# Four PSUM banks for the pairs' products, and a later spread of the next block's roots, in a hybrid decoder layer

## The chip, the cores and the metric

The kernel runs on one core of one Trainium2 chip. The metric is the time of one execution in microseconds (us). Every time below is from the chip: from the timed runs, or from one profiled execution of the kernel before. The engines are named as the profile names them: PE (TensorE, matmul) with PEld (its weight loads), DVE (VectorE), ACT (ScalarE), POOL (GpSimd) and SP (whose queue issues DMAs). PSUM, where matmuls put their sums, has eight banks here, and the kernel uses all eight.

## The reference, cut to what matters

One layer of a decoder, over 2048 prompt tokens and 64 sample tokens. Everything begins with an RMS norm of x and one large projection `w_in`; the three branches' results are weighted by sigmoid gates and summed.

```python
def _mixer_inputs(x, p):
    xn = _rmsnorm(x, p["norm_w"])            # x * rsqrt(mean(x*x) + eps) * w
    h = jnp.einsum("btd,de->bte", xn, p["w_in"])
    ...
    gates = jax.nn.sigmoid(g + p["b_gate"]).reshape(n, t, N_BRANCHES, D_MODEL)

def _merge(x, y_a, y_b, y_c, z_a, z_b, z_c, gates, p):
    a = jnp.einsum("bte,ed->btd", jax.nn.silu(z_a) * y_a, p["w_out_a"])
    b = jnp.einsum("bte,ed->btd", jax.nn.silu(z_b) * y_b, p["w_out_b"])
    c = jnp.einsum("bte,ed->btd", jax.nn.silu(z_c) * y_c, p["w_out_c"])
    m = gates[:, :, 0] * a + gates[:, :, 1] * b + gates[:, :, 2] * c
    return x + jnp.einsum("btd,de->bte", m, p["w_o"])
```

## The kernel before

The tokens are worked through in four blocks: three of 512 tokens, and a last one of 512 prompt and 64 sample tokens (576, in two chunks of 288). Each block goes through the same phases: keys and values, queries, attention and convolution, the chunk MLP, the gate phase, the output phase. Weights are fp32 and each is split into a high part `wh` (a cast on ACT, line 222) and a low part `wl` (a subtraction on DVE, line 223); a product is then three matmuls, `wh`·`xh`, `wh`·`xl` and `wl`·`xh`. The weights come by DMA into a ring of three `raw` tiles and are split two units ahead of use into a ring of four `wh`/`wl` tiles.

The change touches the gate phase. There are 24 gate tiles (8 output tiles for each of 3 branches). The first four are done one by one (`single`): 24 matmuls of 512 columns for the gate, a sigmoid, 12 matmuls for the branch's output (`merge`, lines 231 to 233), which DVE multiplies with the gate (line 897) and adds up (line 903). The other 20 are done in ten pairs (`pair`) by a scheme of the Strassen-Winograd kind, which forms two gate tiles for both halves of the tokens with seven products in place of eight. Each product is 12 matmuls (lines 929 to 931) of half the tokens, 256 columns (288 in the last block). POOL forms the sums of weights that the scheme needs (lines 154 to 164). The seven products, in the order in which PE does them, are named here by their right side: `11`, `t3`, `t2`, `t1`, `21`, `t4`, `22`. Each is put into one PSUM bank and read by additions: `11` by a copy on ACT (line 946), `t3` and `t2` by DVE lines 950 and 949 (949 first, since 950 adds its result), `t1` by 952 and 953, `21` by 955, `t4` by 956, `22` by 959. Before, the banks are S0, pv, S1, S0, S1, pv, S0 in that order; the product that comes to a bank must wait until the one before it in that bank has been read. The other five banks are a ring of three (`ps_mm`, tag `mm`), which the gate and merge matmuls use, and a ring of two (`ps_tp`), for transposes.

During the gate phase the next block's root mean squares are prepared (`xrstd`): per 128 tokens a DMA of x and a sum of squares on ACT (line 261), then the roots on POOL (`fin`, lines 218 and 219), then a spread of the roots over the partitions: transposes on PE (line 275) into `ps_tp`, and a copy on ACT (line 278). The roots are used at the end of the gate phase (line 296). For the block of 576 there are five pieces, the last of 64 tokens.

What sets the order: PE's instructions and the DMAs of SP stand in program order; a scheduler orders DVE, ACT and POOL. Side work is hung into PE's program with `later(delay, piece)`. The clock of these delays counts PE's work: a gate tile of 512 columns is 1.0, a merge 0.5, a product 0.25. `flush()` runs all that is pending at once; one stands in `single(2)`, at 4.0, since what follows needs the third branch.

Of the kernel before, what the change touches and what calls it, by code (L numbers as in the profile page):

```python
# [10 lines left out]
F32 = mybir.dt.float32  # L11
F32R = mybir.dt.float32r
AF = mybir.ActivationFunctionType
ALU = mybir.AluOpType
AX = mybir.AxisListType

P = 128
# [34 lines left out]
def trunk_kernel(ctx: ExitStack, tc: tile.TileContext, A, O):  # L52
# [7 lines left out]
    psum = ctx.enter_context(tc.tile_pool(name="psum", bufs=1, space=bass.MemoryType.PSUM))  # L60

    def ps_mm():
        return psum.tile([P, 512], F32, tag="mm", name="ps_mm", bufs=3)
# [22 lines left out]
    def later(delay, fn):  # L86
        heapq.heappush(pending, (clock[0] + delay, len(pieces)))
        pieces.append(fn)
# [6 lines left out]
    def flush():  # L95
        while pending:
            pieces[heapq.heappop(pending)[1]]()
# [89 lines left out]
    def take(name, j):  # L187
        i = taken[0]
        assert units[i] == (name, j), (units[i], name, j)
        taken[0] += 1  # L190
        split_to(i + 1 + ahead["splits"])
        w = ready[i]
        ready[i] = None
        return w
# [26 lines left out]
    def split(hi, lo, src):  # L221
        nc.scalar.copy(hi, src)  # L222
        nc.vector.tensor_tensor(lo, src, hi.bitcast(F32), ALU.subtract)  # L223

    def gemm_t(ps, w, kts, rh, rl, c0, c1):

        wh, wl = w
        o = ps[:, : c1 - c0]
        for k in range(kts):
            ws = slice(k * P, (k + 1) * P)  # L230
            nc.tensor.matmul(o, wh[:, ws], rh(k, c0, c1), start=k == 0, stop=False)  # L231
            nc.tensor.matmul(o, wh[:, ws], rl(k, c0, c1), start=False, stop=False)  # L232
            nc.tensor.matmul(o, wl[:, ws], rh(k, c0, c1), start=False, stop=k == kts - 1)  # L233
            if k % 2:
                tick((c1 - c0) / 512 * 0.25)
# [12 lines left out]
    def xrstd(sb):  # L248

        t0, _, chunks, _ = SBS[sb]  # L250
        n = chunks[-1][1]
        tiles = [(c, min(c + P, n)) for c in range(0, n, P)]
        st = {}
        st["r"] = res.tile([P, TMAX], F32, tag="acc", name="acc")[:, :n]
        r = small.tile([P, 8], F32, tag="xr", name="xr")

        def piece(j, c0, c1):
            w = c1 - c0
            x = raws.tile([P, WE], F32, tag="raw", name="xraw")[:w]
            nc.sync.dma_start(x, A["xn"][t0 * P + c0:t0 * P + c1])  # L260
            nc.scalar.activation(x, x, AF.Square, accum_out=r[:w, j:j + 1])

        def fin():
            for j0, j1, w in ((0, n // P, P), (n // P, len(tiles), n % P)):
                if w and j1 > j0:
                    rstd(r[:w, j0:j1], r[:w, j0:j1], j1 - j0, D)

        def spread():
            for t in (tiles[:4], tiles[4:]):
                if t:  # L270
                    ps = ps_tp()
                    b = t[0][0]
                    for c0, c1 in t:
                        w = c1 - c0
                        nc.tensor.transpose(
                            ps[:, c0 - b:c1 - b], r[:w, c0 // P:c0 // P + 1].broadcast_to([w, P]), ident[:w, :w]
                        )
                    nc.scalar.copy(st["r"][:, b:t[-1][1]], ps[:, : t[-1][1] - b])

        return st, [lambda j=j, c=c: piece(j, *c) for j, c in enumerate(tiles)] + [fin, spread]  # L280
# [54 lines left out]
    pair = [None]  # L335
# [535 lines left out]
    def keep(new, old):  # L871

        tc.keep_in_program_order(nc.scalar.dma_start(O[new][:, : P - TS, :], A[old][:, TS:, :]))

    def gate_phase(sb, br, xs):
        chunks = SBS[sb][2]
        n = chunks[-1][1]
        h = n // 2
        sums, last_sums = xs
        st = {}  # L880
        if sb + 1 < len(SBS):
            st, xpieces = xrstd(sb + 1)
            for j, p in enumerate(xpieces):
                later(0.5 + 0.75 * j, p)

        def bias(j):
            d, b = divmod(j, 3)
            return bg[:, 8 * b + d:8 * b + d + 1]

        def merge(j, t, wo):  # L890

            d, b = divmod(j, 3)
            brr = (lambda k, x, y: br[b][0][:, k, x:y], lambda k, x, y: br[b][1][:, k, x:y])
            for c0, c1 in chunks:
                pa = ps_mm()
                gemm_t(pa, wo, 4, *brr, c0, c1)
                nc.vector.tensor_tensor(t[:, c0:c1], pa[:, : c1 - c0], t[:, c0:c1], ALU.mult)  # L897
            if b == 0:
                st["acc"] = t
            else:  # L900
                acc = st["acc"]
                out = acc if b == 1 else st["m"][:, d, :n]
                nc.vector.tensor_tensor(out, acc, t, ALU.add)

        def single(j):
            wg = take("wt", 28 + j)
            t = tmp("t", [P, n])
            for c0, c1 in chunks:
                pg = ps_mm()
                gemm_t(pg, wg, KT, *xr, c0, c1)  # L910
                nc.scalar.activation(t[:, c0:c1], pg[:, : c1 - c0], AF.Sigmoid, bias=bias(j))
            if j == 2:
                flush()
                st["m"] = res.tile([P, KT, TMAX], F32, tag="mh", name="m")
                for q in range(2):
                    later(0.25 + 0.75 * q, lambda q=q: last_sums(q))
                if not sb:
                    later(4.0, lambda: keep("sk", "ck"))
                    later(12.0, lambda: keep("sv", "cvr"))
            merge(j, t, take("wout", j))  # L920

        def product(bank, w, half, r):

            o = psum.tile([P, 512], F32, tag=bank, name="pair" + bank, bufs=1)[:, :h]
            wh, wl = w
            rh, rl = sums[r]
            for k in range(4):
                ws = slice(half * H + k * P, half * H + (k + 1) * P)
                nc.tensor.matmul(o, wh[:, ws], rh(k), start=k == 0, stop=False)  # L929
                nc.tensor.matmul(o, wh[:, ws], rl(k), start=False, stop=False)  # L930
                nc.tensor.matmul(o, wl[:, ws], rh(k), start=False, stop=k == 3)  # L931
                if k % 2:
                    tick(h / 2048)
            return o

        def pair(j):

            add = nc.vector.tensor_tensor
            ta, tb, ca, cb = [tmp(x, [P, n]) for x in ("t", "t", "ca", "cb")]
            lo, hi = slice(0, h), slice(h, n)
            p1, u, u3, u5 = ca[:, lo], ca[:, hi], cb[:, lo], cb[:, hi]
            w = take("pair", (28 + j, 0))
            nc.scalar.copy(p1, product("S0", w, 0, "11"))
            p3 = product("pv", w, 1, "t3")
            w = take("pair", (28 + j, 1))
            add(u, product("S1", w, 0, "t2"), p1, ALU.add)  # L949
            add(u3, p3, u, ALU.add)  # L950
            p5 = product("S0", w, 1, "t1")
            add(u5, p5, u, ALU.add)
            add(tb[:, hi], p5, u3, ALU.add)
            w = take("pair", (28 + j, 2))
            add(ta[:, lo], product("S1", w, 0, "21"), p1, ALU.add)
            add(tb[:, lo], product("pv", w, 1, "t4"), u3, ALU.add)
            nc.scalar.activation(tb, tb, AF.Sigmoid, bias=bias(j + 1))
            w = take("pair", (28 + j, 3))
            add(ta[:, hi], product("S0", w, 0, "22"), u5, ALU.add)
            nc.scalar.activation(ta, ta, AF.Sigmoid, bias=bias(j))  # L960
            wh, wl = take("wouts", j)
            if j == 22:

                st["hi"] = res.tile([P, KT, TMAX], F32R, tag="ml", name="mhi")
                st["lo"] = [res.tile([P, 4, TMAX], F32R, tag="br0" + x, name="mlo" + x) for x in "hl"]
                for d in range(KT - 1):
                    part(d)
            merge(j, ta, (wh[:, :H], wl[:, :H]))
            merge(j + 1, tb, (wh[:, H:], wl[:, H:]))

        def part(d):
            split(st["hi"][:, d, :n], st["lo"][d // 4][:, d % 4, :n], st["m"][:, d, :n])

        for j in range(SINGLES):
            single(j)
        for j in range(SINGLES, 24, 2):
            pair(j)
        part(KT - 1)
        flush()
        if sb + 1 < len(SBS):  # L980
            for j, p in enumerate(xsplit(sb + 1, st)):
                later(0.25 + 0.75 * j, p)
        return st["hi"], st["lo"]
# [206 lines left out]
```

## Time and profile before

| | us |
|---|---|
| median of three timed runs | 2015.57 (2015.36 to 2016.91) |
| the profiled execution's own time | 2013.36 |
| its span, first to last instruction | 2011.6 |
| PE busy in the span | 1972.3 (98%) |
| DVE busy | 1365.2 (68%) |
| ACT busy | 945.1 (47%) |
| POOL busy | 335.0 (17%) |

The rows of the profile give an engine's busy time; for PE the ends of matmuls are modelled and overlap, so a wait is read more exactly from the distance between the starts of matmuls. A "wait" in the profile is idle time of an engine that ended with an event of another; PE and PEld are listed apart, so one stop of TensorE can stand in both lists. "Granted clock" is the share of TensorE's full speed: 1.00 is 2.4 GHz, 0.50 is 1.2 GHz.

### The profile page before, as it was taken

How to read it: one execution, taken by the hardware profiler on the slowest of the kernel's cores; microseconds unless marked ns; L12 is line 12 of the kernel's file. 1: busy time of each engine (PE TensorE's matmuls, PEld its weight loads, DVE VectorE, ACT ScalarE, POOL GpSimd, SP SyncE). 2: the span in 40 equal slices, each digit the busy share in tenths (PEclk: the TensorE clock that was granted, in tenths of full speed). 3: DMA queues.
4: the chain of work that ended last, by engine and by line, in shares of the span. 5: the costliest groups of instructions: out<-in, count | busy, mean ns of one | idle time of the engine just before them, and what ended most of it. 6: DMA issues, size and time to landing. Idle time of an engine off the chain costs nothing.

```text
span 2011.6 us, 30272 instructions
## 1 busy us (share of the span) xinstructions
PE 1972.3 (98%) x11771; PEld 1765.4 (88%) x11771; DVE 1365.2 (68%) x2367; ACT 945.1 (47%) x1679; POOL 335.0 (17%) x294
## 2 busy tenths in 40 slices
PE   6999999999999999999999998999999999999999
PEld 5888889998888889998888887999889999999999
DVE  5688377875588558777478736777647873587772
ACT  4775254442576344444367524444347743333340
POOL 2100024320100004440200002442020000133310
PEclk9999999999999999999999998999999999999999
DMA  6222233336222232226322223223622242222233
GB/s 209 90 79 84 84 126 115 102 115 224 95 73 74 94 114 101 101 95 207 129 84 74 87 76 123 97 95 115 229 87 56 62 114 69 71 82 87 95 101 109
DMA packets 85711, 212.44 MB, mean 106 GB/s; under 512 B 18224, under 2 KB 23344, under 8 KB 85552
## 3 DMA queue, kind: packets, MB, share of 16 engines
q1 hardware_dynamic: 85536, 209.53, 32.4%
q8 instruction: 92, 1.51, 0.3%
q10 hardware_dynamic: 32, 0.98, 0.1%
q14 instruction: 51, 0.42, 0.1%
HBM read 201.46 MB, written 10.00 MB: 105 GB/s over the span
## 4 chain that ended last, share of the span: by engine, by line
PE 89%; DVE 5%; ACT 4%; DMA 1%; issue 1%; POOL 1%; SPq 0%; ACTq 0%; DVEq 0%; POOLq 0%
PE ps_mm L231 18%; PE ps_mm L232 18%; PE ps_mm L233 18%; PE pairS L929 4%; PE pairS L930 4%; PE pairS L931 4%; DVE wl L223 3%; PE pairpv L930 2%; PE pairpv L929 2%; PE pairpv L931 2%; PE ps_mm L353 2%; PE ps_mm L352 2%; PE ps_mm L351 2%; ACT wh L222 2%; PE wideS L353 1%; PE wideS L352 1%
## 5 line engine op out<-in xcount | busy, mean ns | idle before, releaser
L223 DVE TENSOR_TENSOR wl<-raw,wh 128x1024 fp32r<-128x1024 f32 (+1 forms) x416 | 461.7, 1118 | 272.1 <-ACT wh L222 269.1
L222 ACT CAST wh<-raw 128x1024 fp32r<-128x1024 f32 (+1 forms) x416 | 354.7, 866 | 539.1 <-PE ps_mm L232 232.7
L231 PE MATMUL ps_mm<-xh,wh 128*128 128x512 f32 (+1 forms) x1280 | 460.2, 360 | 0.0
L233 PE MATMUL ps_mm<-xh,wl 128*128 128x512 f32 (+1 forms) x1280 | 451.7, 353 | 0.0
L232 PE MATMUL ps_mm<-xl,wh 128*128 128x512 f32 (+1 forms) x1280 | 451.6, 353 | 0.0
L233 PEld LDWEIGHTS ps_mm<-xh,wl 128*128 128x128 f32 x1280 | 241.0, 188 | 30.7
L232 PEld LDWEIGHTS ps_mm<-xl,wh 128*128 128x128 f32 x1280 | 241.5, 189 | 27.1
L231 PEld LDWEIGHTS ps_mm<-xh,wh 128*128 128x128 f32 x1280 | 241.3, 189 | 27.3
L222 ACT CAST wh<-s 128x512 fp32r<-128x512 f32 x120 | 70.9, 621 | 194.1 <-PE ps_mm L232 116.5
L929 PE MATMUL pairS<-xh,wh 128*128 128x256 f32 (+1 forms) x480 | 140.1, 292 | 8.1 <-DVE ca L949 7.9
L218 POOL TENSOR_SCALAR vr<-vssq 128x1 f32<-128x1 f32 (+1 forms) x17 | 5.4, 316 | 804.9 <-ACT vn L795 804.5
L931 PE MATMUL pairS<-xh,wl 128*128 128x256 f32 (+1 forms) x480 | 137.2, 286 | 0.0
L930 PE MATMUL pairS<-xl,wh 128*128 128x256 f32 (+1 forms) x480 | 137.1, 286 | 0.0
L231 PE MATMUL ps_mm<-mhi,wh 128*128 128x512 f32 (+1 forms) x320 | 112.5, 352 | 0.9 <-ACT mhi L222 0.9
L233 PE MATMUL ps_mm<-mhi,wl 128*128 128x512 f32 (+1 forms) x320 | 112.5, 352 | 0.0
L897 DVE TENSOR_TENSOR t<-ps_mm,t 128x512 f32<-128x512 f32 (+1 forms) x120 | 70.8, 593 | 58.5 <-PE ps_mm L233 57.3
L929 PEld LDWEIGHTS pairS<-xh,wh 128*128 128x128 f32 x480 | 91.2, 190 | 14.5 <-DVE ca L949 13.2
L154 POOL TENSOR_TENSOR s<-raw 128x512 f32<-128x512 f32 x40 | 56.8, 1419 | 243.1 <-DMA raw<-in_wt 192.2
L164 POOL TENSOR_TENSOR s<-raw,s 128x512 f32<-128x512 f32 x40 | 67.6, 1690 | 160.2 <-DVE wl L223 160.2
L930 PEld LDWEIGHTS pairS<-xl,wh 128*128 128x128 f32 x480 | 91.4, 190 | 1.2
L929 PE MATMUL pairS<-xsum,wh 128*128 128x256 f32 (+1 forms) x320 | 91.7, 287 | 0.0
L930 PE MATMUL pairS<-xsum,wh 128*128 128x256 f32 (+1 forms) x320 | 91.6, 286 | 0.0
(280 smaller groups left out, 4638.7 us busy)
## 6 DMA issues: line engine op xcount, KB each, us to landing
raw<-in_wt SPq DMA_DIRECT2D x208, 512.0 KB
raw<-in_wout SPq DMA_DIRECT2D x96, 256.0 KB
raw<-in_wn SPq DMA_DIRECT2D x40, 512.0 KB
raw<-in_wo SPq DMA_DIRECT2D x32, 512.0 KB
xraw<-in_xn SPq DMA_DIRECT2D x12, 512.0 KB
xt<-in_xt SPq DMA_DIRECT2D x24, 256.0 KB
out_yt<-xt SPq DMA_DIRECT2D x24, 256.0 KB
xbuf<-in_xt SPq DMA_DIRECT2D x16, 256.0 KB
```

The source lines that it names most:

```text
L164: add(combos["s2"], r0[:, H:], combos["s2"], ALU.subtract)
L222: nc.scalar.copy(hi, src)
L223: nc.vector.tensor_tensor(lo, src, hi.bitcast(F32), ALU.subtract)
L231: nc.tensor.matmul(o, wh[:, ws], rh(k, c0, c1), start=k == 0, stop=False)
L232: nc.tensor.matmul(o, wh[:, ws], rl(k, c0, c1), start=False, stop=False)
L233: nc.tensor.matmul(o, wl[:, ws], rh(k, c0, c1), start=False, stop=k == kts - 1)
L352: nc.tensor.matmul(o, xh[:, k, ts], wl, start=False, stop=False)
L353: nc.tensor.matmul(o, xl[:, k, ts], wh, start=False, stop=k == KT - 1)
L897: nc.vector.tensor_tensor(t[:, c0:c1], pa[:, : c1 - c0], t[:, c0:c1], ALU.mult)
L929: nc.tensor.matmul(o, wh[:, ws], rh(k), start=k == 0, stop=False)
L930: nc.tensor.matmul(o, wh[:, ws], rl(k), start=False, stop=False)
L931: nc.tensor.matmul(o, wl[:, ws], rh(k), start=False, stop=k == 3)
```

## The change

Two things. First, product `t1` goes into a buffer of the `mm` ring in place of S0, `21` into S0 in place of S1, and `22` into S1 in place of S0, so that the order of banks is S0, pv, S1, mm, S0, pv, S1. Second, the last two pieces of the next block's preparation (`fin` and the spread) are no longer due at 0.5 + 0.75·j with the others. They are hung in behind the flush of `single(2)`, at 2.0 and 6.0 after it.

```diff
@@ gate_phase
         if sb + 1 < len(SBS):
             st, xpieces = xrstd(sb + 1)
-            for j, p in enumerate(xpieces):
+            for j, p in enumerate(xpieces[:-2]):
                 later(0.5 + 0.75 * j, p)
+            st["roots"] = xpieces[-2:]
...
                 for q in range(2):
                     later(0.25 + 0.75 * q, lambda q=q: last_sums(q))
+
+                for q, p in enumerate(st.get("roots", [])):
+                    later(2.0 + 4.0 * q, p)
...
+        def bank_of(bank):
+            if bank == "mm":
+                return ps_mm()
+            return psum.tile([P, 512], F32, tag=bank, name="pair" + bank, bufs=1)
+
         def product(bank, w, half, r):
 
-            o = psum.tile([P, 512], F32, tag=bank, name="pair" + bank, bufs=1)[:, :h]
+            o = bank_of(bank)[:, :h]
...
-            p5 = product("S0", w, 1, "t1")
+            p5 = product("mm", w, 1, "t1")
...
-            add(ta[:, lo], product("S1", w, 0, "21"), p1, ALU.add)
+            add(ta[:, lo], product("S0", w, 0, "21"), p1, ALU.add)
...
-            add(ta[:, hi], product("S0", w, 0, "22"), u5, ALU.add)
+            add(ta[:, hi], product("S1", w, 0, "22"), u5, ALU.add)
```

Lines from 949 on of the kernel before are nine higher in the changed kernel (949 is 958 there), 929 to 931 are 938 to 940, and 897 and 903 are 898 and 904.

PE at the border between products `t1` and `21`, in the second pair of the first block, before (a name's number tells buffers apart; what an instruction waits for is behind it):

```order
L929 MATMUL pairS_2813<-xsum,wh 128x256
L930 MATMUL pairS_2813<-xsum,wh 128x256
L931 MATMUL pairS_2813<-xsum,wl 128x256
L929 MATMUL pairS_2832<-xh,wh 128x256 [waits DVE_49]
L930 MATMUL pairS_2832<-xl,wh 128x256
L931 MATMUL pairS_2832<-xh,wl 128x256
```

The same place now:

```order
L938 MATMUL ps_mm<-xsum,wh 128x256
L939 MATMUL ps_mm<-xsum,wh 128x256
L940 MATMUL ps_mm<-xsum,wl 128x256
L938 MATMUL pairS_2826<-xh,wh 128x256 [waits Activation_49]
L939 MATMUL pairS_2826<-xl,wh 128x256
L940 MATMUL pairS_2826<-xh,wl 128x256 [waits DVE_49]
```

The first matmul of `21` no longer waits for DVE (line 949, which reads S1) but for ACT; the third waits for DVE's low part of its weights.

DVE in the fifth pair of the first block, before:

```order
L223 TENSOR_TENSOR wl<-s_3234,wh 128x512
L949 TENSOR_TENSOR ca<-pairS_3319,ca 128x256
L223 TENSOR_TENSOR wl<-raw,wh 128x1024
L950 TENSOR_TENSOR cb<-pairpv,ca 128x256
L952 TENSOR_TENSOR cb<-pairS_3334,ca 128x256
```

and now:

```order
L223 TENSOR_TENSOR wl<-s_3234,wh 128x512
L958 TENSOR_TENSOR ca<-pairS_3319,ca 128x256
L223 TENSOR_TENSOR wl<-raw,wh 128x1024
L959 TENSOR_TENSOR cb<-pairpv,ca 128x256
L961 TENSOR_TENSOR cb<-ps_mm,ca 128x256
```

Nothing moved here: only the bank that line 961 reads is another. In the whole program DVE's order differs in one place, nine rows in the third block's sums for `t4` (lines 840 and 864), and POOL's and SP's orders do not differ at all.

PE around the flush of `single(2)` in the third block (the next block has five pieces), before:

```order
L231 MATMUL ps_mm<-xh,wh 128x512
L232 MATMUL ps_mm<-xl,wh 128x512
L233 MATMUL ps_mm<-xh,wl 128x512
L275 MATMUL ps_tp<-c_ident,xr 128x128 x4
L275 MATMUL ps_tp<-c_ident,xr 128x64
L231 MATMUL ps_mm<-br2h,wh 128x512
L232 MATMUL ps_mm<-br2l,wh 128x512
L233 MATMUL ps_mm<-br2h,wl 128x512
```

The transposes now stand in the second pair of that block, between products `21` and `t4`:

```order
L938 MATMUL pairS_11584<-xh,wh 128x256
L939 MATMUL pairS_11584<-xl,wh 128x256
L940 MATMUL pairS_11584<-xh,wl 128x256
L275 MATMUL ps_tp<-c_ident,xr 128x128 x4
L275 MATMUL ps_tp<-c_ident,xr 128x64
L938 MATMUL pairpv<-xsum_11244,wh 128x256
L939 MATMUL pairpv<-xsum_11244,wh 128x256
L940 MATMUL pairpv<-xsum_11244,wl 128x256
```

They moved back by the rest of the singles and most of two pairs, in this block and in the two before it alike; ACT's copies (line 278) moved with them.

## Rows read from the trace of the kernel before

**Rows 1.** The page: span, and busy time of each engine.
```profile
span 2011.6 us, 30272 instructions
PE 1972.3 (98%) x11771; PEld 1765.4 (88%) x11771; DVE 1365.2 (68%) x2367; ACT 945.1 (47%) x1679; POOL 335.0 (17%) x294
```
**Rows 2.** Waits: engine, line, waited for; us in total, times, longest us.
```profile
PEld pairS L929 <- DVE ca L949: 13.2, 25, 1.6
...
PE ps_tp L275 <- POOL xr L219: 7.7, 1, 7.7
```
**Rows 3.** Timeline of PE, start and us: first, fifth and last waiting products.
```profile
297.29 0.39 PE L929 MATMUL pairS<-xh,wh 128*128 128x256 f32 x1 [0.39 <-DVE ca L949]
...
358.17 0.28 PE L929 MATMUL pairS<-xsum,wh 128*128 128x256 f32 x1
...
361.11 0.38 PE L929 MATMUL pairS<-xh,wh 128*128 128x256 f32 x1 [1.35 <-DVE ca L949]
361.33 0.28 PE L930 MATMUL pairS<-xl,wh 128*128 128x256 f32 x1
...
362.64 0.32 PE L929 MATMUL pairpv<-xsum,wh 128*128 128x256 f32 x1
...
1926.06 0.40 PE L929 MATMUL pairS<-xh,wh 128*128 128x288 f32 x1 [0.60 <-DVE ca L949]
```
**Rows 4.** Timeline of DVE in the fifth pair of the first block.
```profile
360.65 0.41 DVE L949 TENSOR_TENSOR ca<-pairS,ca 128x256 f32<-128x256 f32 x1
360.98 1.21 DVE L223 TENSOR_TENSOR wl<-raw,wh 128x1024 fp32r<-128x1024 f32 x1
362.11 0.41 DVE L950 TENSOR_TENSOR cb<-pairpv,ca 128x256 f32<-128x256 f32 x1
```
**Rows 5.** Timeline of PE, DVE and POOL in the eighth pair of the first block.
```profile
406.28 2.33 DVE L223 TENSOR_TENSOR wl<-raw,wh 128x1024 fp32r<-128x1024 f32 x1 [1.99 <-ACT wh L222]
408.54 0.41 DVE L949 TENSOR_TENSOR ca<-pairS,ca 128x256 f32<-128x256 f32 x1
408.98 0.42 DVE L950 TENSOR_TENSOR cb<-pairpv,ca 128x256 f32<-128x256 f32 x1
...
407.49 2.27 POOL L160 TENSOR_TENSOR s<-s,raw 128x512 f32<-128x512 f32 x1
...
409.00 0.38 PE L929 MATMUL pairS<-xh,wh 128*128 128x256 f32 x1 [0.89 <-DVE ca L949]
```
**Rows 6.** Timeline of POOL after the flush in the third block.
```profile
1229.44 1.29 POOL L154 TENSOR_TENSOR s<-raw 128x512 f32<-128x512 f32 x1 [3.47 <-DMA raw<-in_wt]
...
1234.58 0.87 POOL L219 TENSOR_TENSOR xr<-xr,mhalf 64x1 f32<-64x1 f32 x1
```
**Rows 7.** Timeline of PE, and one row of DVE, in the same place.
```profile
1227.23 0.60 PE L275 MATMUL ps_tp<-c_ident,xr 128*128 128x128 f32 x4
1235.50 0.36 PE L275 MATMUL ps_tp<-c_ident,xr 64*128 64x64 f32 x1 [7.67 <-POOL xr L219]
...
1236.39 0.63 PE L232 MATMUL ps_mm<-br2l,wh 128*128 128x512 f32 x1
...
1227.02 0.69 DVE L223 TENSOR_TENSOR br2l<-sp,br2h 128x512 fp32r<-128x512 f32 x1 [0.69 <-ACT br2h L222]
```
**Rows 8.** Stretches: us, busy (instructions) of the engines, granted clock, DMA share, GB/s.
```profile
737.00:926.00 189.00, 188.26 (x1232) 172.21 (x1231) 146.80 (x236) 86.55 (x142) 65.64 (x42) 1.00 0.34 112
...
1231.50:1241.70 10.20, 6.20 (x15) 4.83 (x16) 4.66 (x7) 3.15 (x7) 3.30 (x4) 0.50 0.16 51
```
**Rows 9.** Timeline of PE and DVE at the same flush in the second block.
```profile
754.21 0.60 PE L275 MATMUL ps_tp<-c_ident,xr 128*128 128x128 f32 x4
754.56 0.48 PE L231 MATMUL ps_mm<-br2h,wh 128*128 128x512 f32 x1
755.09 0.50 PE L232 MATMUL ps_mm<-br2l,wh 128*128 128x512 f32 x1
...
754.35 0.69 DVE L223 TENSOR_TENSOR br2l<-sp,br2h 128x512 fp32r<-128x512 f32 x1 [0.69 <-ACT br2h L222]
```

## The prediction

> **What bounds the kernel now.** I read the busy times first. PE is busy for 1972.3 of the 2011.6 us of the span and DVE, the next, for 1365.2 [rows 1]. The change leaves the number of matmuls as it is, so it can win only where TensorE stands still or runs at half clock. Then I read whom TensorE waited for. Two of the rows belong to the code that is edited [rows 2]: weight loads of line 929 waited 25 times, 13.2 us in all, for DVE's line 949, and one transpose of line 275 waited 7.7 us for POOL's line 219. Line 949 is the reader of `t2` in S1, and the waiting product is `21`, which wants S1 next but one. Line 219 makes the roots.
>
> **The banks: what is removed.** In the fifth pair of the first block `t1` begins at 358.17 and `21` at 361.11 [rows 3]. A product is 12 matmuls and lasts 1.44 us (in the last block's 288 columns 1.60) where nothing stops it, so `21` was due at 359.61 and lost 1.50. Its second matmul comes 0.22 us after the first where 0.12 is usual [rows 3]; so a wait also costs a restart of 0.10. Together that is the 1.6 which the waits view gives as the longest [rows 2]. Taken by starts in this way, the 25 waiting products lost 11.9 us and 2.7 for restarts: 14.6 in all, the first 0.55 at 297.29, the last 0.76 at 1926.06 [rows 3]. The waits view's 13.2 is the lower bound of the same thing. I take 14.6, since the span is made of starts.
>
> **The banks: what waits next.** `21` now goes into S0, whose tenant `11` was copied out on ACT four products earlier, and `22` goes into S1, which 949 has read well before. `t1` takes an `mm` buffer; with three buffers and three (last block: five) uses per pair, its tenant is the `t1` or a merge of the pair before, and no merge shows up as waiting for `mm` among TensorE's waits; zero, and if that cover were gone, one DVE step such as 0.41 [rows 4]. The low half of `21`'s weights, for which its third matmul now waits by name, stands ahead of 949 on DVE, so it is done where 949 is merely late. What is left is `t4`: it wants pv, and pv's reader is line 950, directly behind 949 in DVE's order. Where DVE is late, `t4` inherits the lateness less its own 1.44 us. In the fifth pair of the first block a split of 1.21 us stands between 949 and 950, and 950 ends at 362.52 [rows 4], while `t4` would be due at 361.05 (359.61 + 1.44). So all of this pair's 1.6 stays; the wait only moves one product on. In the eighth pair `21` lost 1.05 (409.00 against 407.95) and 950 ends at 409.40 [rows 5], `t4` is due at 409.39: some 0.07 and a restart of 0.10 stay. One more pair (lost 0.99) is at the edge with about 0.1. Otherwise `t2`'s and `t3`'s readers follow each other within 0.5 us and 1.44 covers it. Remaining: 1.6 + 0.3. **Banks: 14.6 - 1.9 = 12.7 us gained.**
>
> Does the clock come into this term? The second block's gate phase has ten pairs, most with short waits, and its granted clock is 1.00 [rows 8]; so I count none. The Trainium skill (TensorE: Matmul & The Clock Gate, "A second HAM failure mode: psum-queue depth-cycling") tells of a kernel that cycles through PSUM banks, whose short idles between groups made the clock go down and up. If each of the 25 waits had cost the 2.65 us found below for a drop, the banks would bring 66 us more. The trace speaks against it.
>
> **The roots: what is removed.** In the third block four transposes run at 1227.23 and the fifth at 1235.50, when POOL's second root pair (64 tokens) ends [rows 6, 7]. POOL came to it late: in its order two weight sums stand ahead, and the first waited until 1229.44 for a DMA [rows 6]. With the transposes gone from here, PE comes straight to the merge, whose second matmul needs `br2l`. DVE finished that at 1227.71 (1227.02 + 0.69), and in the second block that matmul began 0.05 after it, at 755.09 against 755.04 [rows 9]. So it can begin at 1227.76 in place of 1236.39 [rows 7]: 8.63 us. Behind the wait the clock was granted at 0.50 (1.2 GHz) from 1231.5 to 1241.7, and PE had stood idle before the fall [rows 8]. From 1236.39 to 1241.7 are 5.3 us of matmuls at half speed: 2.65 lost. Without the idle time I expect no fall. A restart at 1227.76 takes 0.1 back. **8.63 + 2.65 - 0.1 = 11.2 us gained.**
>
> **The roots: what is added.** Four transposes take 0.35 us of PE (754.21 to 754.56) [rows 9]. At their old place in the first two blocks they stood in front of the wait for `br2l` and cost next to nothing; that wait stays where it is. In the second pair nothing hides them: 0.35 each in blocks one and two, 0.45 for the third block's five: **1.1 us lost.** Do they wait at the new place? POOL's order is unchanged, so the roots are formed where they were, and in the third block they end at 1234.58 [rows 6], some 30 us before the new place is reached there. ACT's copies move too; what queues behind one on ACT are weight casts for products a pair away, so I put them at 0, with the 0.57 us of such a copy as the upper bound. No DMA is moved: the pieces that load x keep their due times, and SP's order is the same.
>
> **Sum.** 12.7 + 11.2 - 1.1 = 22.8 us. The span goes from 2011.6 to 1988.8, the profiled execution from 2013.36 to 1990.6. That execution lies 2.2 below the median of the timed runs; off the median of 2015.57 the forecast is **1992.8 us**.
>
> **Rivals.**
> *The wait moves to `t4` in most pairs.* Ahead of 949 stands the split of the merge's weights, 1024 columns. It takes 1.21 us [rows 4], but 2.33 while POOL's sums run beside it [rows 5]. PE's order of work changes where the two meet. If the long form met every pair, each `t4` would wait like the eighth pair's, 0.17 us: 40 × 0.17 = 6.8 back, and 1992.8 + 6.8 = 1999.6. For it: three pairs already have lost around 1 us behind the long form. Against it: DVE and POOL are paced by PE through the weight ring, and most pairs lost a third of a microsecond only. The Trainium skill (SBUF — State Buffer, "SBUF: two separate sides") says that DVE with two SBUF inputs and POOL share a port pair as an exclusive lock, the loser waiting for the whole instruction; by that rule the split can wait up to one POOL sum. The 2.33 beside the 2.27 of POOL's line 160 agrees.
> *The weights come late instead.* If PE, unbroken, outruns the splits, the banks' 12.7 comes back as waits for `wl`: 2005.5. Against it: DVE is busy 146.80 of 189 us in that gate phase and ACT 86.55 [rows 8], and pairs without any wait already follow one another in the first block.
> *The spread waits at its new place (slower).* It would have to find the roots unready in all three blocks, POOL being over 25 us later than now, held by its weight sums and their DMA. Then each block has a wait of 7.7 and a clock loss of 2.65, 31 us in place of 10.3: 20.7 more, less the 12.7 of the banks, plus 1.1: about 2024.7. POOL's unchanged order speaks against it.
> *More than forecast.* The fifth pair's wait goes too and the transposes find a gap: 14.6 + 11.2 = 25.8, 1989.8.
> *The change does not do what it says.* The roots are in fact formed no later, and if `t1`'s buffer made it wait as S1 did, only the roots' 10.1 would remain: 2005.5, the time of the second rival, and I count it there.
>
> **How the numbers follow.** Forecast, within 1.5 or so, 0.70; more than forecast 0.07; `t4` 0.12; weights late or no gain from the banks 0.07; slower 0.04. A measurement of this kernel tells about 0.2% (4 us) from no change, so all cases but the last are faster. Faster 0.94; the same 0.03, for a mixture of the second rival with part of the third; slower 0.03. The range takes in the forecast, the greater gain and the first rival, with a little for the spread of the runs below: 1989.0 to 2000.0.
>
> **What would show it.** Right: the row of line 929's (now 938) waits for 949 (958) gone from `21`; in its place a few waits of `t4` for line 959, the longest about 1.5 us in the first block's fifth pair, under 3 us in all. No stop before the merge at the third block's flush over 0.5 us, and a granted clock of 1.00 there. The transposes in the second pair start without a wait. Wrong: waits of line 938 of 6 us or more in sum, any wait of a matmul for line 223 in the pairs beyond a few tenths, a transpose that waits for POOL, or a new stretch at 0.50.

## The result and the profile after

| | before | after |
|---|---|---|
| median of the timed runs, us | 2016.24 (2015.36 to 2018.06, 4 runs) | 1990.69 (1989.59 to 1991.92, 4 runs) |
| ratio, 95% interval | | 0.9872 [0.986, 0.9884] |
| the profiled execution's own time | 2013.36 | 1990.79 |
| its span | 2011.6 | 1989.0 |

The change makes the kernel 1.3% faster. The forecast was 1992.8 (1989.0 to 2000.0) for the time and 1988.8 for the span.

The page of after, span and busy time, beside [rows 1]: the count of matmuls is the same, and PE's busy time is now nearer to the span.

```profile
span 1989.0 us, 30333 instructions
PE 1964.0 (99%) x11771; PEld 1761.0 (89%) x11771; DVE 1363.8 (69%) x2367; ACT 945.3 (48%) x1679; POOL 332.5 (17%) x294
```

Waits of TensorE in after (engine, line, waited for; us in total, times, longest), those that answer to [rows 2]. The 25 waits of product `21` for `t2`'s reader are gone, and so is the transpose's wait of 7.7 us for POOL. One wait of `t4` is left for its bank (line 959, 950 before), with a second in PEld's list; and the flushes now show short waits for `br2h` and `br2l`, which the transposes used to stand in front of.

```profile
PE pairpv L938 <- DVE cb L959: 1.4, 1, 1.4
PEld pairpv L938 <- DVE cb L959: 1.8, 2, 1.6
PE ps_mm L231 <- ACT br2h L222: 0.7, 1, 0.7
PE ps_mm L232 <- DVE br2l L223: 0.6, 3, 0.2
```

Timeline of PE, then DVE, in the fifth pair of the first block of after (answers to [rows 3, 4]; start and us). `21` begins at 359.95, 1.44 behind `t1` at 358.51: no stop. The split of 1.21 us still stands between 958 and 959, 959 ends at 362.86, and `t4`, due at 361.39, begins at 362.92.

```profile
358.51 0.28 PE L938 MATMUL ps_mm<-xsum,wh 128*128 128x256 f32 x1
...
359.95 0.28 PE L938 MATMUL pairS<-xh,wh 128*128 128x256 f32 x1
...
362.92 0.38 PE L938 MATMUL pairpv<-xsum,wh 128*128 128x256 f32 x1 [1.37 <-DVE cb L959]
```
```profile
360.99 0.41 DVE L958 TENSOR_TENSOR ca<-pairS,ca 128x256 f32<-128x256 f32 x1
361.32 1.21 DVE L223 TENSOR_TENSOR wl<-raw,wh 128x1024 fp32r<-128x1024 f32 x1
362.45 0.41 DVE L959 TENSOR_TENSOR cb<-pairpv,ca 128x256 f32<-128x256 f32 x1
```

Timeline at the third block's flush in after: PE, then DVE's low part, then POOL's last root (answers to [rows 6, 7]). Between the last gate matmul and the merge's second there is now 0.23 us of waiting, where 7.67 us and a run at half clock stood. POOL still forms the last root late: it ends at 1232.58, 8.6 us behind the flush. Nothing on PE asks for it there any more; the five transposes stand at 1258.45 and take 0.73 until `t4` at 1259.18.

```profile
1223.74 0.39 PE L233 MATMUL ps_mm<-xh,wl 128*128 128x512 f32 x1
1223.97 0.50 PE L231 MATMUL ps_mm<-br2h,wh 128*128 128x512 f32 x1
1224.70 0.50 PE L232 MATMUL ps_mm<-br2l,wh 128*128 128x512 f32 x1 [0.23 <-DVE br2l L223]
...
1258.45 0.80 PE L275 MATMUL ps_tp<-c_ident,xr 128*128 128x128 f32 x5
1259.18 0.39 PE L938 MATMUL pairpv<-xsum,wh 128*128 128x256 f32 x1
```
```profile
1223.95 0.69 DVE L223 TENSOR_TENSOR br2l<-sp,br2h 128x512 fp32r<-128x512 f32 x1 [0.69 <-ACT br2h L222]
```
```profile
1232.04 0.54 POOL L219 TENSOR_TENSOR xr<-xr,mhalf 64x1 f32<-64x1 f32 x1
```

Why the last root is late stands on ACT as well as on POOL. Three of POOL's weight sums come first (lines 154, 155 and 160). ACT's cast of line 222 waits 4.38 for line 155, the sum of squares of the 64 tokens (line 261) stands behind that cast on ACT, and POOL, done with its sums at 1230.76, waits another 0.54 for it. The kernel before has the same order, with 2.76 and 0.56. ACT, then POOL, in after:

```profile
1229.53 0.62 ACT L222 CAST wh<-raw 128x512 fp32r<-128x512 f32 x1 [4.38 <-POOL raw L155]
1230.06 1.06 ACT L261 ACTIVATE xraw<-xraw 64x1024 f32<-64x1024 f32 x1
```
```profile
1231.29 0.66 POOL L218 TENSOR_SCALAR xr<-xr 64x1 f32<-64x1 f32 x1 [0.54 <-ACT xraw L261]
```

**Where the time went, stretch by stretch.** The stretches are cut at starts of matmuls: from the first matmul of the first pair to the first matmul of the last pair's `22` (four rows, one per block), from there to the first pair of the third block, and from there again to the first pair of the fourth. Columns: stretch and length, busy us (instructions) of PE, PEld, DVE, ACT and POOL, granted clock, DMA share, GB/s. Before, then after:

```profile
290.98:443.52 152.54, 149.73 (x1045) 140.30 (x1044) 116.61 (x182) 67.08 (x111) 57.57 (x37) 1.00 0.33 111
765.92:916.86 150.94, 150.25 (x1046) 140.32 (x1044) 113.98 (x181) 66.56 (x111) 58.89 (x37) 1.00 0.31 105
1249.57:1402.84 153.27, 150.54 (x1045) 140.29 (x1044) 112.14 (x177) 64.42 (x107) 59.17 (x36) 1.00 0.31 103
1776.15:1946.86 170.71, 168.86 (x1263) 167.39 (x1261) 127.97 (x193) 65.94 (x107) 57.12 (x36) 1.00 0.28 93
916.86:1249.57 332.71, 324.46 (x1555) 271.00 (x1554) 218.76 (x380) 164.83 (x294) 24.72 (x34) 0.98 0.34 109
1402.84:1776.15 373.31, 371.57 (x2517) 348.86 (x2515) 240.62 (x447) 183.30 (x340) 25.41 (x36) 1.00 0.33 97
```
```profile
291.57:442.37 150.80, 149.43 (x1050) 140.49 (x1049) 117.10 (x181) 67.75 (x112) 57.36 (x37) 1.00 0.33 112
764.14:913.23 149.09, 149.09 (x1050) 140.37 (x1049) 113.41 (x182) 67.13 (x112) 59.26 (x37) 1.00 0.32 107
1235.49:1385.20 149.71, 149.71 (x1050) 140.54 (x1049) 114.12 (x183) 67.20 (x113) 59.84 (x37) 1.00 0.32 106
1756.98:1924.21 167.23, 167.23 (x1262) 167.23 (x1261) 128.66 (x193) 66.03 (x107) 56.37 (x36) 1.00 0.28 94
913.23:1235.49 322.26, 321.45 (x1551) 268.34 (x1549) 214.49 (x376) 161.72 (x288) 22.91 (x33) 1.00 0.34 112
1385.20:1756.98 371.78, 370.01 (x2516) 347.26 (x2515) 240.50 (x447) 183.53 (x340) 25.46 (x36) 1.00 0.32 98
```

The pairs took 627.46 us in all and now take 616.83: 10.63 less, the banks' gain less the transposes. The stretch with the third block's flush is 10.45 shorter. The stretch up to the fourth block's pairs is 1.53 shorter, although the change touches nothing in it; that is looked into below. The rest is small: 0.59 lost before the first pair, 0.63 won between the first block's pairs and the second's, 0.03 lost behind the last pair. Together 10.63 + 10.45 + 1.53 + 0.63 - 0.59 - 0.03 = 22.6, the difference of the spans.

### The profile page after: what moved, and what is told of

Same layout as the page of the kernel before. It is cut to its first block, busy times and chain, and to the rows that moved or that the text cites. A ratio compares the mean times of both kernels' runs of the same rounds, so it can differ in the third digit from the quotient of the medians.

```text
span 1989.0 us, 30333 instructions
## 1 busy us (share of the span) xinstructions
PE 1964.0 (99%) x11771; PEld 1761.0 (89%) x11771; DVE 1363.8 (69%) x2367; ACT 945.3 (48%) x1679; POOL 332.5 (17%) x294
## 4 chain that ended last, share of the span: by engine, by line
PE 92%; ACT 3%; DVE 2%; DMA 1%; issue 1%; POOL 0%; SPq 0%; ACTq 0%; DVEq 0%
PE ps_mm L232 18%; PE ps_mm L231 18%; PE ps_mm L233 18%; PE pairS L940 4%; PE pairS L939 4%; PE pairS L938 4%; PE pairpv L938 2%; PE pairpv L939 2%; PE pairpv L940 2%; PE ps_mm L353 2%; PE ps_mm L352 2%; PE ps_mm L351 2%; PE wideS L351 1%; PE wideS L353 1%; PE wideS L352 1%; PE ps_tp L573 1%
## 5 line engine op out<-in xcount | busy, mean ns | idle before, releaser
L940 PEld LDWEIGHTS pairS<-xh,wl 128*128 128x128 f32 x480 | 91.5, 191 | 0.0
L223 DVE TENSOR_TENSOR wl<-s,wh 128x512 fp32r<-128x512 f32 x120 | 84.5, 728 | 5.9 <-ACT wh L222 3.6
```

## Experiments

Every edit is one to the changed kernel. Times are medians with the range of the runs; the ratio is against the kernel before on the same chip. "By starts" is the method of the prediction: how much later a matmul begins than its neighbours' usual distance says.

**1. The banks alone.** The roots' pieces go back to their old due times.

```diff
-            for j, p in enumerate(xpieces[:-2]):
+            for j, p in enumerate(xpieces):
                 later(0.5 + 0.75 * j, p)
-            st["roots"] = xpieces[-2:]
...
-                for q, p in enumerate(st.get("roots", [])):
-                    later(2.0 + 4.0 * q, p)
```

> The changed order of banks alone; the roots' pieces as in the kernel before. Theory (the two parts are separate stops of TensorE and add up): the 25 waits of product 21 are gone and a few waits of t4 for pv's reader remain, under 3 us in sum, the longest about 1.5 us in the first block's fifth pair; the third block's fifth transpose still waits 7 to 8 us for POOL and a stretch of about 10 us at half clock follows. Span about 2011.6 - 11.9 = 1999.7 us, the time about 12 us under the kernel before. Rival (weights late: PE, unbroken, waits for its split weights instead): new waits for line 223 in the pairs, span over 2008.

Measured: 2000.63 (1999.47 to 2002.03), ratio 0.993 [0.9918, 0.9942], span 2000.1. Waits of PE:

```profile
PE ps_tp L275 <- POOL xr L219: 9.3, 1, 9.3
...
PE pairpv L934 <- DVE cb L955: 1.4, 1, 1.4
```

The waits of `21` are gone with the banks alone, `t4` keeps its one, and the stretch with the third block's flush is as long as before (333.67 from 912.35 to 1246.02). The two halves of the change do not need each other.

**2. The roots alone.** The banks go back.

```diff
-            p5 = product("mm", w, 1, "t1")
+            p5 = product("S0", w, 1, "t1")
...
-            add(ta[:, lo], product("S0", w, 0, "21"), p1, ALU.add)
+            add(ta[:, lo], product("S1", w, 0, "21"), p1, ALU.add)
...
-            add(ta[:, hi], product("S1", w, 0, "22"), u5, ALU.add)
+            add(ta[:, hi], product("S0", w, 0, "22"), u5, ALU.add)
```

> The later roots alone; the banks as in the kernel before. Theory: no wait of a transpose and no half-clock stretch in the third block's gate phase; product 21 still waits about 25 times for line 949 (here under a later number), 12 to 16 us in all. Span about 2011.6 - 9.5 = 2002 us, the time about 10 us under the kernel before. If the parts add up, the gains of this run and of the one with the banks alone make that of the whole change, 22.6 us of span, within 2 us. Rival (PE meets another wait at the flush, such as the third block's first weights): a gain of 5 us or less.

Measured: 2005.65 (2003.03 to 2009.11), ratio 0.9955 [0.9943, 0.9966], span 2005.4. Waits of PEld, and the stretch with the third block's flush:

```profile
PEld pairS L938 <- DVE ca L958: 17.3, 26, 1.5
```
```profile
921.25:1243.28 322.03, 321.29 (x1551) 268.29 (x1549) 214.30 (x376) 161.84 (x288) 22.57 (x33) 1.00 0.35 112
```

The flush stretch has its whole gain (322.03). The bank waits are all there, 17.3 in the waits view where 12 to 16 were expected, 19.0 by starts where the profile of before has 14.6, which is why the span lies 3 us above the 2002 expected. The gains of experiments 1 and 2 by medians, 13.9 and 8.9 against 2014.5 on that chip, add up to 22.7. Those by spans (11.5 and 6.2) fall 4.9 short of the whole change's 22.6, of which 4.4 is what this execution's bank waits had more than the first profile of before.

**3. One more buffer, but `21` stays in S1.** `t1` stays in the ring, `21` and `22` go back to their old banks. It tells "one more bank" from "another neighbour".

```diff
             p5 = product("mm", w, 1, "t1")
...
-            add(ta[:, lo], product("S0", w, 0, "21"), p1, ALU.add)
+            add(ta[:, lo], product("S1", w, 0, "21"), p1, ALU.add)
...
-            add(ta[:, hi], product("S1", w, 0, "22"), u5, ALU.add)
+            add(ta[:, hi], product("S0", w, 0, "22"), u5, ALU.add)
```

The roots' pieces go back as in experiment 1.

> Four banks go round, but 21 stays in S1 and 22 in S0, only t1 goes to the mm ring; roots as before. Theory (what costs is that 21 wants the bank that t2's late reader holds, not how many banks there are): the waits of 21 stay, 12 to 16 us in 20 to 28 times, and the span stays within 2 us of 2011.6, the time within 3 us of the kernel before. Rival (a fourth bank as such relieves the pairs, for instance because DVE reads t1 more freely): span near that of the run with the banks alone, 1999.7.

Measured: 2018.61 (2016.76 to 2019.99), ratio 1.0016 [1.0007, 1.0025], span 2017.0. A fourth buffer by itself wins nothing: `21` still waits for the reader of `t2` in S1. What the theory missed is that it came out slower. Waits of `21`, and the first of them with DVE's 954 (949 before):

```profile
PE pairS L934 <- DVE ca L954: 11.0, 20, 1.4
```
```profile
298.40 0.36 PE L934 MATMUL pairS<-xh,wh 128*128 128x256 f32 x1 [0.24 <-DVE ca L954]
```
```profile
297.84 0.41 DVE L954 TENSOR_TENSOR ca<-pairS,ca 128x256 f32<-128x256 f32 x1
```

954 ends at 298.25 and `21` begins 0.15 later; before, in the fifth pair, 949 ended at 361.06 and `21` began 0.05 later, at 361.11 [rows 3, 4]. In this kernel the first matmul of `21` waits for two semaphores, DVE's and ACT's (the list of weight loads puts ten of these stops down to ACT's line 222, `wh`), where it waited for one. The trace shows how: in 26 of the 27 waiting pairs an instruction of its own, `EVENT_SEMAPHORE`, takes DVE's semaphore ahead of the weight load. It lasts 0.05 us, and `21` begins 0.15 behind DVE's end in all 26. In the 27th, the first pair of the last block, there is none, and `21` begins 0.05 behind it. The instructions of line 934 of this kind (shortest, median and longest in ns), then `21` and line 954 in that one pair:

```profile
L934 PEldq EVENT_SEMAPHORE  x115: 51/51/51, 298.3 to 1949.1; - x115
```
```profile
1787.22 0.40 PE L934 MATMUL pairS<-xh,wh 128*128 128x288 f32 x1 [0.33 <-DVE ca L954]
```
```profile
1786.72 0.45 DVE L954 TENSOR_TENSOR ca<-pairS,ca 128x288 f32<-128x288 f32 x1
```

The second matmul is 0.07 late in the 26, in place of 0.10, so such a stop costs 0.06 more than one that waits for a single semaphore: 1.6 us in all. By starts the waits come to 18.2 and their restarts to 2.65, 6 us more than in the first profile of before. The other 4 or so lie within what these waits vary by in kernels with the old neighbours (14.6 and 16.5 by starts in the two profiles of before, 19.0 in experiment 2). So the later start explains a part of the 4.1 us between the medians, and the rest stays open.

**4. Only the 64 tokens' transpose moves.** Four banks as in the change; the roots and the four large transposes stay where the kernel before has them, and the fifth transpose with its copy is hung in 6.0 behind the flush.

```diff
-        def spread():
-            for t in (tiles[:4], tiles[4:]):
+        def spread(part):
+            for t in part:
...
+        st["tail"] = (lambda: spread([tiles[4:]])) if tiles[4:] else None
...
-                for q, p in enumerate(st.get("roots", [])):
-                    later(2.0 + 4.0 * q, p)
+                if st.get("tail"):
+                    later(6.0, st["tail"])
```

> The four banks, and of the roots' pieces only one is moved: in the third block the transpose of the 64 tokens' root and its copy come 6.0 behind the flush; everything else of the roots is where it was before. Theory (the whole loss at the flush was that one transpose, which waited for POOL's second root pair, and the four others were ready and hidden in front of the wait for br2l): no wait at the flush over 0.6 us, no half clock there, and 0.7 to 1.2 us less than the changed kernel, since 12 transposes are no longer paid for in the pairs: span 1987.8 to 1988.5. Rival (the four transposes or ACT's copy of them hold the flush up too): a wait of 2 us or more at the third block's flush, span over 1991.

Measured: 1989.53 (1988.43 to 1991.02), ratio 0.9875 [0.9861, 0.9889], span 1987.7. PE at the flush:

```profile
1222.98 0.60 PE L275 MATMUL ps_tp<-c_ident,xr 128*128 128x128 f32 x4
1223.33 0.47 PE L231 MATMUL ps_mm<-br2h,wh 128*128 128x512 f32 x1
```

The merge's second matmul follows at 1223.72, with no wait to speak of, and the stretch with the flush takes 321.95 us (322.26 in the changed kernel). The whole gain of the roots comes from one transpose of 64 columns. The other twelve of the three blocks cost next to nothing at their old place, in front of a wait that is there anyway, and something at the new.

**5. The same transpose, 1.0 behind the flush in place of 6.0.** A dose of the suspected cause, POOL's lateness: experiment 4 with one number changed.

```diff
-                    later(6.0, st["tail"])
+                    later(1.0, st["tail"])
```

> As the kernel with the tail alone, but the 64-token transpose of the third block is due 1.0 after the flush in place of 6.0, so it stands about 5 to 6 us behind the last gate matmul. Theory (what the old place cost is the time until POOL has formed the last root, which it does 8.2 to 8.6 us after that matmul, whatever PE does): the transpose waits 2 to 3.5 us for POOL's line 219, time 2 to 3.5 us above the kernel with the tail at 6.0 if the clock stays at 1.00, and up to 2.7 us more if a stretch at 0.50 follows. Rival (the cost came from standing in the flush, ahead of the merge, and not from the root's time): no wait for line 219, time within 0.7 us of the kernel with the tail at 6.0.

Measured: 1993.43 (1992.85 to 1995.12), ratio 0.9899 [0.9884, 0.9913], span 1991.7. PE, then POOL, then the stretch behind (columns as above; from 1224 to 1230 the clock was 1.00):

```profile
1221.97 0.60 PE L275 MATMUL ps_tp<-c_ident,xr 128*128 128x128 f32 x4
...
1230.33 0.27 PE L275 MATMUL ps_tp<-c_ident,xr 64*128 64x64 f32 x1 [2.12 <-POOL xr L219]
```
```profile
1229.74 0.54 POOL L219 TENSOR_TENSOR xr<-xr,mhalf 64x1 f32<-64x1 f32 x1
```
```profile
1230.50:1235.00 4.50, 4.50 (x14) 3.52 (x14) 4.42 (x8) 0.89 (x3) 1.64 (x1) 0.62 0.27 101
```

The root ends 8.3 us behind the flush here (1230.28 against 1221.97), as in the kernel before (1235.45 against 1227.23) and in the changed one (8.6): its time does not hang on where PE asks. The transpose that asks earlier waits for the rest, 2.12 us, and a stretch at 1.2 GHz follows it. From the four transposes to the first pair are 15.7 us (1221.97 to 1237.71), in experiment 4 11.5 (1222.98 to 1234.51): 4.2 more, of which the wait is half.

**6. `t4` to the ring as well.**

```diff
-            add(tb[:, lo], product("pv", w, 1, "t4"), u3, ALU.add)
+            add(tb[:, lo], product("mm", w, 1, "t4"), u3, ALU.add)
```

> The changed kernel with one more product, t4, put into a buffer of the mm ring in place of pv, so that it no longer waits for line 959. Theory (what the banks still cost after the change are t4's waits and restarts alone, 2.76 us by the starts of matmuls): no product of a pair waits for a reader any more, the rows of line 938 for line 959 are gone, span 1989.0 - 2.8 = 1986.2, time about 1988. Rival (the fifth pair's lateness of DVE is only handed on, to the next product or to the mm ring, which now has two of seven products in it): a wait of 1 to 1.5 us stands at 22, at t4 for mm or at the next pair, and the span stays within 0.7 us of 1989.0.

Measured: 1989.16 (1988.54 to 1990.67), ratio 0.9878 [0.9861, 0.9895], span 1987.2. No product waits for a bank in either list of waits. The stretch of the first block's pairs (the second's is as long, the third's 149.30, the fourth's 167.23), and the one up to the fourth block's:

```profile
290.99:439.91 148.92, 148.92 (x1049) 140.28 (x1048) 116.19 (x181) 67.45 (x112) 55.78 (x37) 1.00 0.34 113
...
1381.91:1755.23 373.32, 371.58 (x2517) 348.79 (x2515) 240.47 (x447) 183.41 (x340) 25.41 (x36) 1.00 0.32 97
```

The pairs take 614.37 us, 2.46 less than in the changed kernel: that is what the banks still cost there. The span fell by 1.8 only, since this execution has the longer form of the last stretch (373.32, after has 371.78). The rival, the lateness handed on, is out: PE is busy in the whole of each block's pairs. This rests on the trace; the timed runs, from two chips, overlap (1988.54 to 1990.67 here, 1989.59 to 1991.92 for the changed kernel).

**7 and 8. Both, and the changed kernel beside it.** The diffs of experiments 4 and 6 together: the tail's transpose alone behind the flush, and `t4` in the ring.

> The kernel with only the 64-token transpose moved behind the flush (fin and the spread of the four large pieces stay where the kernel before has them), and t4 in the mm ring too. Theory: both gains are independent and add up: 1987.7 (the kernel with the tail alone) less the 2.8 us of t4's waits is a span of about 1985, a time of 1986.5 to 1987. Rival (the two are the same slack, handed on): span 1987.5, time 1989.3.

Measured: 1988.44 (1986.85 to 1989.54), ratio 0.9872 [0.9857, 0.9887], span 1987.1. It lies between theory and rival, so it was run again, beside the changed kernel as it is, on one chip:

> The kernel with the tail's transpose alone behind the flush and t4 in the mm ring, beside the changed kernel on the same chip. Theory: it saves what is left of the waits and the four large transposes per block in the pairs, 616.83 - 613.08 = 3.75 us there, and 0.5 us at the third block's flush, less what the half-clock stretch in the attention of the last block adds in some runs (1.5): a median 2 to 4 us below the changed kernel's. Rival (these gains are slack handed on): medians within 1 us of each other.

> The changed kernel, unchanged, timed beside the next one on the same chip and profiled again. Theory (its pairs lose the fifth pair's wait and little else, the same in each run, and a stretch of some 3.4 us at half clock in the last block's attention comes in some runs and not in others, whatever the kernel): the ten pairs of the four blocks take 616 to 617.5 us together as in the first profile (616.83), and from the last product of the third block to the first of the fourth PE takes either 371.8 or 373.3 us, nothing between. Time 1990 to 1992.

Measured: 1988.07 (1986.28 to 1988.59), ratio 0.9865 [0.9848, 0.9881], span 1986.2; the changed kernel 1990.64 (1990.07 to 1992.69), ratio 0.9881 [0.9866, 0.9896], span 1988.6. The two ranges do not meet: 2.6 us less. The stretch of the first block's pairs in the new kernel (the third's, with the one transpose, is 148.86), and the one up to the fourth block's (371.75 in the changed kernel's second profile):

```profile
291.45:439.94 148.49, 148.49 (x1045) 139.87 (x1044) 118.12 (x182) 67.04 (x111) 55.34 (x37) 1.00 0.35 114
...
1380.89:1754.23 373.34, 371.59 (x2517) 348.80 (x2515) 240.45 (x447) 183.27 (x340) 25.43 (x36) 1.00 0.33 97
```

148.49 us, which the second block takes too, is the floor: ten pairs with no stop and no transpose. The fourth block's is 167.23, here and in the changed kernel. Four blocks at the floor make 3 × 148.49 + 167.23 = 612.70, and every kernel can be set against it. This kernel, the fastest here, needs 613.07; the changed kernel needs 616.83, and 616.50 in its second profile.

**9. The kernel before, once more,** without an edit.

> The kernel before, unchanged, profiled once more: its times vary by several us from run to run, those of the changed kernel by two. Theory (the variation is the bank waits, whose size depends on how DVE and POOL happen to stand to each other): against the profile that was shown first (span 2011.6, 14.6 us of waits of 21 by the starts), the difference in span is the difference in those waits, to within 1 us; the transpose's wait for line 219 and its stretch at half clock stay at 7 to 10 us and 10 us. Rival (the variation is in the roots' wait, or in the clock elsewhere): the waits of 21 stay within 1 us of 14.6 and the span differs by more than that.

Measured: 2012.75, span 2011.0. Its bank waits (the transpose's wait for line 219 is 7.3), and its stretch up to the fourth block's pairs:

```profile
PEld pairS L929 <- DVE ca L949: 15.1, 25, 1.5
```
```profile
1404.15:1775.93 371.78, 370.01 (x2517) 347.27 (x2515) 240.51 (x447) 183.26 (x340) 25.39 (x36) 1.00 0.32 98
```

Both expectations fell in their strict form. The bank waits do vary: 13.2 in the waits view of the first profile [rows 2], 15.1 here; by starts 1.9 us more. But the span is 0.6 shorter, since the last stretch has its short form (371.78 against 373.31) and the flush stretch is 0.9 shorter. Three things vary between runs of one kernel, and the bank waits are one.

## Why the prediction was right, point by point

| term | forecast | measured | from |
|---|---|---|---|
| lost at the banks before | 14.6 | 14.76 | 627.46 - 612.70 |
| still lost at the banks | 1.9 | 2.46 | 616.83 - 614.37 (experiment 6); 2.4 by starts |
| banks | 12.7 | 12.3 | |
| roots, wait and clock | 11.2 | 10.45 | 332.71 - 322.26 |
| transposes at the new place | -1.1 | -1.67 | 614.37 - 612.70 |
| not forecast | 0 | 1.5 | the stretch up to the fourth block's pairs; the others cancel |
| sum | 22.8 | 22.6 | |

The mechanism was right, but that the span came out only 0.2 off is luck in part. The three terms that were forecast measured 21.1 in place of 22.8, 1.7 less, and the stretch up to the fourth block's pairs, in which the change touches nothing, gave 1.5 back.

**The banks.** The fifth pair's `t4` was to keep 1.6: it begins 1.53 late, with 0.10 for the restart. The eighth pair's was to keep 0.07 and 0.10: it kept 0.05 and 0.10. One more pair was put at 0.1. What the step left out are three small waits, of 0.13 and 0.09 in the third block and 0.05 in the second, and restarts: six second matmuls of `t4` come 0.07 to 0.10 late, three of them behind a first that is 0.05 late or not at all. By starts that is 1.85 + 0.58 = 2.4. Experiment 6 takes all of it away.

**The roots.** Right in its mechanism: experiment 4 moves only the late transpose and has the gain, experiment 5 gives part of the wait and of the half clock back. The merge's second matmul began 0.06 behind the end of `br2l` (1224.70 against 1223.95 + 0.69), where 0.05 was forecast. The prediction put the late root down to two weight sums on POOL; the rows above show three, and ACT's sum of squares behind them as what POOL waited for last. That changes nothing in the sum, since the change takes the asking away and not the lateness. The term came out 0.75 short. From the first instruction behind the gate matmuls to the first pair were 22.34 us (1227.23 to 1249.57 [rows 7]), now 11.52 (1223.97 to 1235.49): 10.8 gained at the place itself. 0.2 of the missing 0.4 is `br2l`, which ends 0.67 behind that point now (1224.64 against 1223.97) and ended 0.48 behind it before (1227.71 against 1227.23). The other 0.4 went in the singles and chunk MLP ahead of the flush. In kernels with the old order the whole stretch varies by more than that (331.80, 332.71, 333.67).

**The transposes.** 0.43 in each of the first two blocks (148.92 - 148.49) and 0.81 in the third (149.30 - 148.49), not 0.35 and 0.45. A break of the matmul stream costs a restart each time: behind the five transposes `t4`'s second matmul comes 0.22 after its first (1259.18 and 1259.40), 0.12 is usual. In the first two blocks it comes 0.20 after. The forecast charged a restart at the merge and none here; and the third block's five transposes took 0.73 up to `t4` (1258.45 to 1259.18), where 0.45 was put. No matmul of the pairs waited behind ACT's copies.

**The rivals.** `t4` waits in most pairs: no, three starts late by 1.8 in all. Weights late: no wait of a pair's matmul for line 223. Spread waits at the new place: it does not. The granted clock is 1.00 in all eight pair stretches of before and after, with the bank waits and without them. The Trainium skill (TensorE: Matmul & The Clock Gate, "A second HAM failure mode: psum-queue depth-cycling") tells of short idles between groups of matmuls that cycle through PSUM banks and make the clock go down and up; here they did not, so that loss was not there to be won back.

**What the sum did not hold.** The stretch up to the fourth block's pairs was 373.31 in the first profile and 371.78 after. The difference is a few microseconds at half clock in the last block's attention, behind two stops of 0.82 and 0.73 us at lines 580 and 581. Those stops stand in every kernel alike; the clock fell behind them in some executions and not in others. The two stops and the stretch around them in experiment 6, where the clock fell (mean granted clock 0.79); then the stretch in the changed kernel, where the same two matmuls waited 0.82 and 0.73 as well, at 1511.73 and 1512.96, and it did not:

```profile
1508.43 0.50 PE L580 MATMUL pv<-rbuf,vst 128*128 128x512 f32 x1 [0.82 <-ACT rbuf L222]
1509.66 0.50 PE L581 MATMUL pv<-rbuf,vst 128*128 128x512 f32 x1 [0.73 <-DVE rbuf L223]
```
```profile
1508.00:1516.00 8.00, 6.83 (x38) 6.47 (x39) 5.16 (x12) 4.88 (x8) 0.00 (x0) 0.79 0.00 0
```
```profile
1505.00:1520.00 15.00, 13.45 (x99) 12.66 (x99) 9.37 (x21) 11.62 (x24) 0.00 (x0) 1.00 0.17 44
```

It fell in six of the twelve profiles: in one of the two of the kernel before, in neither of the changed kernel's, in both of the fastest one's. So the 1.5 us are no part of the change. What decides it in a run stays open.

**The median.** The forecast time was 2.1 above the measured one although the span was 0.2 off. The step that failed is the carrying over of the 2.2 us between the profiled execution and the median. That gap was the draw of one execution, not a constant of the program: 35 timed runs of the kernel before, on all chips, lie between 2011.19 and 2019.12 with a median of 2015.09, while eight of the changed kernel lie between 1989.59 and 1992.69. Off the medians the gain is 24.4 us, off the two profiles 22.6. The kernels with the new banks all keep within 2.1 to 3.3 us (4 to 8 runs each); of those with the old neighbours, the kernel before varies by 7.9 (35 runs), experiment 2 by 6.1 (6 runs) and experiment 3 by 3.2 (10 runs). The bank waits may cause a part of the spread: 14.8 and 16.7 us are lost at the banks in the two profiles of before. But experiment 3 has the largest waits and varies no more than the kernels with the new banks, so it isn't shown.

## What to carry to other kernels

Follow a wait from the waiting instruction to the buffer's reader, and then to what stands behind that reader in its engine's order: here one late DVE addition stopped PE at S1, and the addition behind it was bound to stop it at pv in just the pair where a long split stood between the two. Give a product the bank whose last reader ran longest ago; one more buffer with the old neighbour wins nothing (experiment 3); new neighbours without the extra buffer were not run. Move only the piece that waits: one 64-column transpose carried the whole gain of the roots, and the work moved with it cost 1.3 us, since it had been standing in front of a wait.

## What the runs showed of the hardware

- A matmul that waited for one semaphore began 0.05 to 0.06 us after the end of DVE's instruction. Where it waited for two, one of them in an instruction of its own of 0.05 us, it began 0.15 after it (26 stops of experiment 3, against the one stop of the same trace without that instruction).
- A stop of the matmul stream costs some 0.10 us more at the second matmul, which comes 0.22 after the first where 0.12 is usual; it holds for waits too short to stand in the list. Behind transposes that wait for nothing it is 0.08 (four) or 0.10 (five), and 0.07 in the stops of experiment 3 with two semaphores.
- The same two stops below 1 us, with matmuls between them, are followed by 1.2 GHz in some executions and not in others, 1.5 us apart in time.
- A wait of 2.12 us on PE at full clock was followed by a stretch of 4.5 us with a mean granted clock of 0.62; the place became 4.2 us longer, twice the wait (experiment 5).
